# State-space gate: column tiles outside, both halves of y on chip, the y·silu(z) product formed earlier, and two PSUM banks for the attention's filler

## The chip, the cores and the metric

The kernel runs on one core of one Trainium2 chip. Its time is the device time of one execution in microseconds (us), from runs that alternate between the kernels compared; lower is better. TensorE (PE) does the matmuls, VectorE (DVE), ScalarE (ACT) and GpSimd (POOL) the elementwise work, and SyncE (SP) issues the DMAs. "Span" is the time from the first to the last instruction in one profiled execution.

## The reference

One decoder layer on x of 1024 tokens × 2048 channels, all in float32. The part that the change touches is the state-space gate and what reads it.

```python
h = rms_norm(x, ln_gain)
q, k, v, z_att, u, z_ssm, g_att, g_ssm = jnp.split(h @ w_in, splits, axis=-1)
q, k = rms_norm(q, q_norm_gain), rms_norm(k, k_norm_gain)     # per head and map, 64 wide
...
attn = diff_attention(q, k, v, lam)       # 8 heads: softmax(q1 k1) - lam * softmax(q2 k2), causal
y_att = rms_norm(attn, subln_gain) * (1.0 - lam_init) * silu(z_att)
y = gelu(Re(C scan(u)) + d_skip * u)      # 1024 wide
y_ssm = y * sigmoid(y @ w_glu + b_glu)    # the gate, w_glu 1024 x 1024
y_ssm = y_ssm * silu(z_ssm)
merged = sigmoid(g_att) * (y_att @ w_proj_att) + sigmoid(g_ssm) * (y_ssm @ w_proj_ssm)
x = x + merged @ w_out
```

## The kernel before

Every float32 product is made of three matmuls: each operand is split into a high part (ACT, `split`, line 90) and a low part (DVE or POOL, line 91), and high·high, high·low and low·high are summed in PSUM. Tiles have 128 partitions × 512 columns; tokens come in two halves `t` of 512. Intermediate results go through DRAM buffers (`d_yg` holds y, `d_zs` silu(z_ssm), `d_ys` the gate's result in two parts, `d_k` the raw keys, `d_ks` their normalised parts).

In order of time, the program has these stages. Times are from the span's start.

- To 1060 us: half of the input projection (`part`), together with the scan that makes y and stores it to `d_yg`.
- 1060 to 1741.5 us: the other half, 36 column pairs (`whole`, line 492) in the order q, k, v, za (4 pairs each), zs (4), ga (8), gs (8). A pair is 84 matmuls. DVE and POOL recombine sums with terms reloaded from `d_p` (lines 520, 571 to 582) and combine weights (lines 346, 366); each finished tile goes to an evacuation function. For za and zs that is `evac_gate` (lines 1030 to 1039): ACT takes the sigmoid, POOL multiplies (L1035), SP stores. From the first za pair on, `norms_k` (line 1004 onward) takes a step per pair in program order: load a tile of k (`ks`) and its row factors (`rb`), multiply (DVE, L1015), split, store, 16 steps in all. Its tile has the tag "ks" with one buffer.
- 1741.5 to 1859 us: the gate. For each half t: load and split y's half (`ya`, 8 tiles); for each of 8 column tiles ct: load and split two blocks of `w_glu`, load y (`r`, L1127) and silu(z) (`z`, L1129), multiply them on POOL (L1130), 24 matmuls into `pg` (L1135), sigmoid (ACT, L1137), times r (DVE, L1138), split, two stores to `d_ys` (L1142). Between them `first_head` loads the attention's first head.
- 1859 to 2236 us: attention, 8 heads × 8 blocks of 128 query rows. PE's order is written out by hand: scores `s` (L1178, L1181), and later, at set lags, transposes `tp` (L1203), `values` into `op` (L1215) and `sums_of` into `osm` (L1232). DVE (L1185, L1191 to L1194) and ACT (L1187) do the softmax between them. Into the gaps go `FILL` steps of a filler per block: the matmuls of y_ssm @ w_proj_ssm, 24 for a tile (`ps_tile`, L288), each tile into one bank of PSUM, `ac2`; a tile is emptied by one DVE multiply with `z` (L292). `op` and `osm` take turns in another bank, `tps` "op".
- To 2292 us the filler's rest and its last 3 tiles (`TAIL`), then two full-rate matmul stages to the end.

Outside the hand-written stretch a scheduler sets each engine's order from the program's order, its priorities and its buffers. Every engine runs its own list in order and waits on semaphores. DMAs are all issued by SP, in its order.

Of the kernel before, what the change touches and what calls it, by code (L numbers as in the profile page):

```python
# [19 lines left out]
P = 128  # L20
# [47 lines left out]
def hybrid_block(ctx: ExitStack, tc: tile.TileContext, x_t, x_n, w_t, w_v, w_glu, w_pa, w_ps,  # L68
# [205 lines left out]
    def bank(pool, tag="pc"):  # L274
        return lambda: pool.tile([P, 512], F32, name="pc", tag=tag)
# [20 lines left out]
    def branch_weights():  # L296

        def blocks():
            for n in range(2 * KT):
                for b in range(2):  # L300
                    yield load_w(w_ps[n % KT, :, 4 * b:4 * b + 4], 4, Q if n < 2 * KT - TAIL else V)
        it = blocks()
        queue = [next(it)]

        def take():
            queue.append(next(it, None))
            return queue.pop(0)
        return take
# [17 lines left out]
    with ExitStack() as pa_ctx:  # L326
# [170 lines left out]
        def finish():  # L497

            if pending:
                pending.pop()()  # L500
# [526 lines left out]
            split(hi, lo, tp)  # L1027
            store2([d[h, :, t * 512:(t + 1) * 512] for d in d_vs], hi, lo)

        def evac_gate(dst, silu):  # L1030
# [10 lines left out]
        evacs = {"q": evac_q, "k": evac_k, "v": evac_v, "za": evac_gate(d_za, True), "zs": evac_gate(d_zs, True),  # L1041
                 "ga": evac_gate(d_ga, False), "gs": evac_gate(d_gs, False)}
        first = {kind: i for kind, i, _ in KINDS}
        for i, (kind, n) in enumerate(order):
            f, m = evacs[kind], n - first[kind]
            whole(n, a, 0, lambda c, t, st, f=f, m=m: f(2 * m + c, t, st), qp, None, w)
            w = None
            if n == 8:
                steps = qk_norms()
            if n in (8, 10, 12):  # L1050
                next(steps, None)
            if i == 12:
                ks = norms_k()
            if i >= 12:
                next(ks, None)
        finish()
        ev_ctx.close()
        hp_ctx.close()
# [38 lines left out]
        gl = gl_ctx.enter_context(tc.tile_pool(name="gl", bufs=3))  # L1097
        heads = {}

        def first_head():  # L1100
# [1 line left out]
                yield  # L1102
        head0 = first_head()

        def yg_inputs(t):
            def ld(k, hi, lo):
                r = wp.tile([P, 512], F32, name="ya", tag="value", bufs=2)
                D.dma_start(r, d_yg[k, :, t * 512:(t + 1) * 512])
                split(hi, lo, r)
            return ld  # L1110

        for t in range(2):
            tk = slice(t * 512, (t + 1) * 512)
            ya = act_half(act, yg_inputs(t))
            for ct in range(8):
                for _ in range(2 if 8 * t + ct > 2 else 0):
                    next(head0, None)
                ws = []
                for b in range(2):
                    raw = wp.tile([P, 4, P], F32, name="w_raw", tag="w_raw", bufs=5)  # L1120
                    D.dma_start(raw, w_glu[ct, :, 4 * b:4 * b + 4])
                    m = (2 * ct + b) % 7
                    hi, lo = (wp.tile([P, 4, P], F32R, name=n, tag=f"{n}{m}") for n in ("w_hi", "w_lo"))
                    split(hi, lo, raw)
                    ws.append((hi, lo))
                r = gl.tile([P, 512], F32, name="r", tag="r")
                D.dma_start(r, d_yg[ct, :, tk])  # L1127
                z = gl.tile([P, 512], F32, name="z", tag="z")
                D.dma_start(z, d_zs[ct, :, tk])  # L1129
                Q.tensor_tensor(r, r, z, ALU.mult)  # L1130
                ps = acc.tile([P, 512], F32, name="pg", tag="acc")
                for k in range(8):
                    wh, wl = (x[:, k % 4] for x in ws[k // 4])
                    for n, (x, y) in enumerate(((wh, ya[0][k]), (wh, ya[1][k]), (wl, ya[0][k]))):
                        T.matmul(ps, lhsT=x, rhs=y, start=(k == 0 and n == 0), stop=(k == 7 and n == 2))  # L1135
                sg = gl.tile([P, 512], F32, name="sg", tag="sg", bufs=2)
                A.activation(sg, ps, AF.Sigmoid, bias=sm[:, C_BGLU + ct:C_BGLU + ct + 1])  # L1137
                V.tensor_tensor(r, r, sg, ALU.mult)  # L1138
                hi, lo = (gl.tile([P, 512], F32R, name=n, tag=n, bufs=2) for n in ("yh", "yl"))
# [3 lines left out]
                if t == 1 and ct == 5:  # L1143
                    ps_weights = branch_weights()
        run(head0)
        gl_ctx.close()

# [4 lines left out]
    ssq = const.tile([P, H, NT], F32, name="ssq")  # L1152
    with ExitStack() as at:
        at.enter_context(kq_ctx.pop_all())
        pex = at.enter_context(tc.tile_pool(name="pex", bufs=2))
        wtp = at.enter_context(tc.tile_pool(name="wtp", bufs=1))
        osp = at.enter_context(tc.tile_pool(name="osp", bufs=2))
        tiny = at.enter_context(tc.tile_pool(name="tiny", bufs=6))
        ssp = at.enter_context(tc.tile_pool(name="ssp", bufs=2, space=PSUM))
# [77 lines left out]
        def put(i, f):  # L1237
            late.append((i, f))
            late.sort(key=lambda a: a[0])

        def drain(i):
            while late and late[0][0] <= i:
                late.pop(0)[1]()

        def filler():
            psa0 = act_half(act, finished(d_ys, 0))
            for ct in range(KT):
                yield from ps_tile(0, ct, psa0, bank(ac2), ps_weights)
            psa.append(act_half(act, finished(d_ys, 1)))
            for ct in range(KT - TAIL):  # L1250
                yield from ps_tile(1, ct, psa[0], bank(ssp, "s") if ended and ct % 2 else bank(ac2), ps_weights)

        psa, ended = [], []
        fill = filler()
# [3 lines left out]
        def feed(n):  # L1258

            owed[0] += n  # L1260
            while owed[0] > 0:
                owed[0] -= 1
                if next(fill, 0):
                    return
        with tc.manual_schedule(engines={T.engine}):
            for h in range(H):
                ld = heads.get(h) or load_head(h)
                wts = [[wtp.tile([P, 4 * qb + 4, 512], F32R, name=n, tag=f"{n}{qb}") for n in ("wth", "wtl")]
                       for qb in range(2)]
                for n, tt in enumerate(ORDER):  # L1270
                    i = h * NT + n
                    qb = tt // 4
                    w = weights(i, h, tt, ld)
                    q = FILL[n]
                    put(i + LAG_T, lambda a=(tt, w, wts[qb]): transpose_w(*a))
                    if tt % 4 == 3:
                        def vals(i=i, h=h, qb=qb, wt=wts[qb], ld=ld):
                            sq = values(h, qb, wt, ld)
                            put(i + LAG_V + LAG_S, lambda: sums_of(h, qb, sq))
                        put(i + LAG_V, vals)  # L1280
                    drain(i + 0.1)
                    feed(q - q // 2)
                    drain(i + 0.5)
                    feed(q // 2)
                    drain(i + 0.9)
            ended.append(1)
# [153 lines left out]
```

## Time and profile before

| | us |
|---|---|
| median of 3 runs (2804.27 to 2805.68) | 2805.34 |
| the profiled execution | 2804.28 |
| its span | 2802.5 |
| PE busy in the span | 2695.5 (96%) |
| DVE, ACT, POOL busy | 1844.1, 1205.9, 743.7 |
| gate, 1741.5 to 1859: length, PE busy | 117.5, 100.41 |
| from za's first pairs to zs's last, 1250 to 1452: length, PE busy | 202, 180.00 |
| ga and gs, 1452 to 1741.5: length, PE busy | 289.5, 289.50 |

PE's busy time is modelled from pipelined matmuls, so a busy PE may still run at half rate; the granted clock says so. Idle time is told with the instruction that ended it and the one that released it.

### The profile page before, as it was taken

The page shows a single profiled execution, that of the slowest core. Times are in us where ns is not written, and L with a number is a line of the kernel's source. Part 1 is how long each engine was busy: PE and PEld are TensorE (multiplying, and loading weights), DVE is VectorE, ACT ScalarE, POOL GpSimd, SP SyncE. Part 2 cuts the span into 40 slices and gives each one's busy share as a digit, 9 for nine tenths or more (in the row PEclk, how much of TensorE's full clock was granted, in tenths as well). Part 3 has the DMA queues.
Part 4 walks back from the last instruction along what each step waited for, and adds up shares of the span by engine and source line. Part 5 has one row for each costly group of instructions (what it writes and reads, how often), then busy time and mean ns, then how long its engine had stood idle before and what let it go on. Part 6 is the DMA issues. An engine that isn't in the chain of part 4 may idle for free. (4 is left out here: it accounts for less than half of the span.)

```text
span 2802.5 us, 37947 instructions
## 1 busy us (share of the span) xinstructions
PE 2695.5 (96%) x12402; PEld 2205.5 (79%) x12402; DVE 1844.1 (66%) x3512; ACT 1205.9 (43%) x2359; POOL 743.7 (27%) x1101
## 2 busy tenths in 40 slices
PE   9999999999999998998899999789999999999999
PEld 8888788887878876776678888667878778888887
DVE  4998877777787776787676666457666575325432
ACT  6433455545455544433444444345555433223221
POOL 0002866565674011224442222212222200000000
PEclk9999999999999999999999999999999999999999
DMA  9653333333333454457765555976777386455453
GB/s 350 220 180 115 103 113 117 115 116 120 121 101 117 166 181 165 149 174 230 243 214 167 168 162 169 317 234 194 198 238 206 128 296 194 131 155 177 150 158 113
DMA packets 261926, 487.82 MB, mean 174 GB/s; under 512 B 33912, under 2 KB 44480, under 8 KB 261728
## 3 DMA queue, kind: packets, MB, share of 16 engines
q1 hardware_dynamic: 261728, 485.40, 53.7%
q8 instruction: 98, 1.61, 0.2%
q14 instruction: 100, 0.82, 0.1%
HBM read 345.72 MB, written 139.56 MB: 173 GB/s over the span
## 5 line engine op out<-in xcount | busy, mean ns | idle before, releaser
L492 PE MATMUL acc<-ah,w_hi 128*128 128x512 f32 x2128 | 841.6, 396 | 28.1 <-ACT u L523 22.8
L492 PE MATMUL acc<-ah,w_lo 128*128 128x512 f32 x2128 | 841.0, 396 | 0.0
L492 PE MATMUL acc<-al,w_hi 128*128 128x512 f32 x2128 | 840.2, 395 | 0.0
L90 ACT ACTIVATE w_hi<-w_raw 128x512 fp32r<-128x512 f32 x532 | 333.9, 629 | 523.3 <-PE o L1356 219.7
L91 DVE TENSOR_TENSOR w_lo<-w_raw,w_hi 128x512 fp32r<-128x512 f32 x474 | 338.4, 715 | 308.9 <-ACT w_hi L90 296.3
L492 PEld LDWEIGHTS acc<-ah,w_hi 128*128 128x128 f32 x2128 | 402.7, 189 | 120.6 <-ACT u L523 27.6
L492 PEld LDWEIGHTS acc<-ah,w_lo 128*128 128x128 f32 x2128 | 402.5, 189 | 87.7 <-issue 5.4
L492 PEld LDWEIGHTS acc<-al,w_hi 128*128 128x128 f32 x2128 | 402.9, 189 | 83.4 <-issue 2.0
L90 ACT ACTIVATE w_hi<-value 128x512 fp32r<-128x512 f32 x304 | 191.7, 630 | 313.3 <-DVE value L346 161.4
L91 DVE TENSOR_TENSOR w_lo<-value,w_hi 128x512 fp32r<-128x512 f32 x304 | 219.5, 722 | 61.3 <-ACT w_hi L90 53.7
L1356 PE MATMUL o<-w_lo,mh 128*128 128x512 f32 x512 | 199.2, 389 | 0.0
L1356 PE MATMUL o<-w_hi,ml 128*128 128x512 f32 x512 | 199.2, 389 | 0.0
L1356 PE MATMUL o<-w_hi,mh 128*128 128x512 f32 x512 | 195.3, 389 | 0.0
L581 POOL TENSOR_TENSOR u<-u,q 128x512 f32<-128x512 f32 x72 | 99.8, 1387 | 230.2 <-ACT u L514 120.7
L346 DVE TENSOR_TENSOR value<-w_raw 128x512 f32<-128x512 f32 x152 | 150.3, 989 | 2.7
L1185 DVE TENSOR_SCALAR_CACHE_REDUCE pe<-s,nrq 128x128 f32<-128x128 f32 (+7 forms) x128 | 100.1, 813 | 70.9 <-PE s L1181 58.9
L91 POOL TENSOR_TENSOR w_lo<-w_raw,w_hi 128x512 fp32r<-128x512 f32 x58 | 84.0, 1448 | 234.3 <-ACT w_hi L90 204.0
L575 POOL TENSOR_TENSOR p<-p,q 128x512 f32<-128x512 f32 x36 | 60.5, 1680 | 322.5 <-DVE acc L520 210.0
L288 PE MATMUL pc<-ah,w_hi 128*128 128x512 f32 x256 | 107.6, 420 | 25.4 <-DVE z L292 16.8
L1187 ACT ACTIVATE pe<-pe,mx 128x128 f32<-128x128 f32 (+7 forms) x128 | 98.5, 773 | 42.2 <-DVE pe L1185 42.0
L1356 PEld LDWEIGHTS o<-w_lo,mh 128*128 128x128 f32 x512 | 96.1, 188 | 20.0
L1356 PEld LDWEIGHTS o<-w_hi,mh 128*128 128x128 f32 x512 | 96.1, 188 | 19.9
(681 smaller groups left out, 4588.5 us busy)
## 6 DMA issues: line engine op xcount, KB each, us to landing
w_raw<-in_w_t_dram SPq DMA_DIRECT2D x288, 256.0 KB
q<-d_p SPq DMA_DIRECT2D x160, 256.0 KB
w_raw<-in_w_out_dram SPq DMA_DIRECT2D x128, 256.0 KB
d_p<-u SPq DMA_DIRECT2D x72, 256.0 KB
w_raw<-in_w_ps_dram SPq DMA_DIRECT2D x64, 256.0 KB
w_raw<-in_w_pa_dram SPq DMA_DIRECT2D x64, 256.0 KB
d_p<-ps SPq DMA_DIRECT2D x52, 256.0 KB
d_p<-p SPq DMA_DIRECT2D x36, 256.0 KB
```

The costliest lines, as they stand in the source:

```text
L90: A.activation(hi, src, AF.Copy)
L91: (eng or V).tensor_tensor(lo, src, hi.bitcast(F32), ALU.subtract)
L288: T.matmul(ps, lhsT=w[:, k % 4], rhs=b[k], start=(k == 0 and n == 0), stop=(k == 7 and n == 2))
L346: V.tensor_tensor(t, x, y, ALU.add)
L492: T.matmul(ps, lhsT=x[:, c], rhs=y[i][j], start=(start and j == 0 and n == 0), stop=(j == 3 and n == 2), skip_group_check=True)
L575: e.tensor_tensor(u, u, other(1), ALU.add)
L581: e.tensor_tensor(u, u, other(i), ALU.subtract)
L1185: V.tensor_scalar(pc[c][:, 0:w], sc[c][:, 0:w], nrq[:, 2 * h + c, tt:tt + 1], None, ALU.mult, ALU.min, accum_out=mx[:, c:c + 1])
L1187: ins = A.activation(pc[c][:, 0:w], pc[c][:, 0:w], AF.Exp, bias=mx[:, c:c + 1], scale=-1.0, accum_out=su[:, c:c + 1])
L1356: T.matmul(ps[i], lhsT=a[k][:, tt], rhs=w[:, 0], start=(k == 0 and n == 0), stop=(k == KT - 1 and n == 2))
```

## The change

Four things, beside a longer list of names:

1. The evacuation of zs also loads y from `d_yg` (a tile "y" in the one buffer "ks") and multiplies on DVE, so that `d_zs` holds y·silu(z). The gate then loads one tile per step in place of two, and POOL's multiply there goes.
2. In the gate ct is the outer loop and t the inner: each block of `w_glu` is loaded and split once. Both halves of y stay on chip, the second in the attention's q, k and v tiles (`pairs`), split into them before the loop. The first weights and the first half of y are written ahead of the last evacuations (`finish()`).
3. The filler's tiles take turns between `ac2` and the bank "op", the latter only at steps where no `values` or `sums_of` is near; `give_bank` finishes a tile that still holds it. After the last head they alternate between the score banks and `ac2`. `FILL` falls from 76 to 74 per head; the 16 steps left over run after the last head.
4. The pool `wtp` is opened before `pex`, so that the two lie at other addresses.

```diff
-FILL = (10, 9, 10, 9, 10, 9, 10, 9)
+FILL = (10, 9, 9, 9, 10, 9, 9, 9)
...
                     A.activation(sg, st, AF.Sigmoid)
+                    if src is not None:
+                        y = stg.tile([P, 512], F32, name="y", tag="ks", bufs=1)
+                        D.dma_start(y, src[i, :, t * 512:(t + 1) * 512])
+                        V.tensor_tensor(st, st, y, ALU.mult)
                     Q.tensor_tensor(st, st, sg, ALU.mult)
...
+        ahead = gate_weights(0)
+        ya = act_half(act, yg_inputs(0, lambda: wp.tile([P, 512], F32, name="ya", tag="value", bufs=2)))
         finish()
...
-        for t in range(2):
-            tk = slice(t * 512, (t + 1) * 512)
-            ya = act_half(act, yg_inputs(t))
-            for ct in range(8):
-                for _ in range(2 if 8 * t + ct > 2 else 0):
+        pairs = [kq.tile([P, 2, 512], F32R, name="y2", tag=x) for x in
+                 ("qs0", "kh0", "kl0", "qs1", "kh1", "kl1", "vh", "vl")]
+        ya = [ya, ([x[:, 0] for x in pairs], [x[:, 1] for x in pairs])]
+        load = yg_inputs(1, lambda: gl.tile([P, 512], F32, name="ya", tag="ya", bufs=4))
+        for k in range(8):
+            load(k, ya[1][0][k], ya[1][1][k])
+        for ct in range(8):
+            ws, ahead = ahead, gate_weights(ct + 1) if ct < 7 else None
+            for t in range(2):
+                tk = slice(t * 512, (t + 1) * 512)
+                if 2 * ct + t > 1:
                     next(head0, None)
...
-                r = gl.tile([P, 512], F32, name="r", tag="r")
-                D.dma_start(r, d_yg[ct, :, tk])
-                z = gl.tile([P, 512], F32, name="z", tag="z")
-                D.dma_start(z, d_zs[ct, :, tk])
-                Q.tensor_tensor(r, r, z, ALU.mult)
+                r = gl.tile([P, 512], F32, name="r", tag="r", bufs=3)
+                D.dma_start(r, d_zs[ct, :, tk])
...
+        wtp = at.enter_context(tc.tile_pool(name="wtp", bufs=1))
         pex = at.enter_context(tc.tile_pool(name="pex", bufs=2))
-        wtp = at.enter_context(tc.tile_pool(name="wtp", bufs=1))
...
+        def filler_bank():
+            turn[0] ^= 1
+            if ended:
+                return bank(ssp, "s")() if turn[0] else bank(ac2)()
+            own[0] = bool(turn[0]) and (at_step[0] < NT - 2 or not 0.2 < at_step[0] % NT < 4.3)
+            return bank(tps, "op")() if own[0] else bank(ac2)()
...
+        def give_bank():
+
+            while own[0]:
+                owed[0] -= 1
+                step()
...
                         def vals(i=i, h=h, qb=qb, wt=wts[qb], ld=ld):
+                            give_bank()
                             sq = values(h, qb, wt, ld)
-                            put(i + LAG_V + LAG_S, lambda: sums_of(h, qb, sq))
+                            put(i + LAG_V + LAG_S, lambda: (give_bank(), sums_of(h, qb, sq)))
```

Three places show what this does to the engines' lists.

DVE in the zs pairs, before. `value` and `w_lo` prepare weights, `u2`, `u3`, `p1` and `q` are the tiles that an evacuation takes:

```order
L346 TENSOR_TENSOR value_14648<-w_raw_14620,w_raw_14624 128x512
L91 TENSOR_TENSOR w_lo_14651<-value_14648,w_hi_14650 128x512
L1015 TENSOR_TENSOR ks_16167<-ks_16167,rb_16169 128x512
L346 TENSOR_TENSOR value_14812<-w_raw_14800,w_raw_14802 128x512
L582 TENSOR_TENSOR u3_14592<-acc_14566,u3_14592 128x512
L91 TENSOR_TENSOR sl__16334<-ks_16167,sh__16333 128x512
L91 TENSOR_TENSOR w_lo_14809<-w_raw_14802,w_hi_14808 128x512
L576 TENSOR_TENSOR p1_14496<-acc_14498,p1_14496 128x512
```

And after:

```order
L582 TENSOR_TENSOR u3_14427<-acc_14401,u3_14427 128x512
L91 TENSOR_TENSOR w_lo_14659<-w_raw_14652,w_hi_14658 128x512
L1038 TENSOR_TENSOR u3_14427<-u3_14427,y_14433 128x512
L1015 TENSOR_TENSOR ks_14445<-ks_14445,rb_14447 128x512
L576 TENSOR_TENSOR p1_14322<-acc_14324,p1_14322 128x512
L91 TENSOR_TENSOR w_lo_14494<-value_14472,w_hi_14493 128x512
L91 TENSOR_TENSOR sl__14632<-ks_14445,sh__14631 128x512
L346 TENSOR_TENSOR value_14664<-value_14662,w_raw_14654 128x512
L582 TENSOR_TENSOR u2_14337<-acc_14401,u2_14337 128x512
L91 TENSOR_TENSOR w_lo_14498<-w_raw_14462,w_hi_14497 128x512
L91 TENSOR_TENSOR w_lo_14667<-value_14664,w_hi_14666 128x512
L1038 TENSOR_TENSOR p1_14322<-p1_14322,y_14547 128x512
```

Each zs pair has four multiplies by y (L1038) and one step of `norms_k` (L1015, `sl`) in DVE's list, 22 instructions from one `u3` to the next, and these five loads share one buffer. Before, all 16 steps of `norms_k` stood in the za and zs pairs; now 4 stand in za, 4 in zs and 8 in ga.

DVE at the gate's end, with what an instruction waits for, before: the last product with the sigmoid (L1138), its split, and the first softmax (L1185).

```order
L91 TENSOR_TENSOR yl_18391<-r_18357,yh_18390 128x512 [waits DMAHW4_49,Activation_49]
L1138 TENSOR_TENSOR r_18408<-r_18408,sg_18438 128x512 [waits Activation_49,Pool_49]
L91 TENSOR_TENSOR yl_18442<-r_18408,yh_18441 128x512 [waits DMAHW7_49,Activation_49]
L1185 TENSOR_SCALAR pe_18480,mx_18483<-s_18484,nrq_11008 128x640 [waits DMAHW3_49,DMAHW4_49,DMAHW2_49,DMAHW5_49,DMAHW1_49,DMAHW6_49,DMAHW0_49,DMAHW7_49,DVE_49,PE_49]
L1185 TENSOR_SCALAR pe_18481,mx_18483<-s_18485,nrq_11008 128x640 [waits PE_49]
```

And after:

```order
L91 TENSOR_TENSOR yl_18300<-r_18269,yh_18299 128x512 [waits DMAHW4_49,Activation_49]
L1151 TENSOR_TENSOR r_18307<-r_18307,sg_18334 128x512 [waits DMAHW5_49,Activation_49]
L1198 TENSOR_SCALAR pe_18376,mx_18379<-s_18380,nrq_11008 128x640 [waits PE_49]
L91 TENSOR_TENSOR yl_18338<-r_18307,yh_18337 128x512 [waits DMAHW4_49,Activation_49]
L1198 TENSOR_SCALAR pe_18377,mx_18379<-s_18381,nrq_11008 128x640 [waits PE_49]
```

The first softmax tile no longer waits for eight DMA semaphores (they guarded the gate's buffers, at whose address `pe` lay).

SP at the start of the attention's sixth head, before. `qs`, `kh`, `kl` and `vh`, `vl` are that head's tiles, `ah` and `al` the second half of the gate's result for the filler:

```order
L1068 DMA qs_20732<-d_q1_74 64x1024
L293 DMA d_ps_89<-z_20522 128x512
L97 DMA w_raw_20871<-in_w_ps_dram 128x512
L314 DMA al_20793<-d_ys1_88 128x512
L314 DMA ah_20785<-d_ys0_87 128x512
L314 DMA ah_20786<-d_ys0_87 128x512
L314 DMA al_20794<-d_ys1_88 128x512
L314 DMA ah_20787<-d_ys0_87 128x512
L314 DMA al_20795<-d_ys1_88 128x512
L1068 DMA kh_20733<-d_k0_75 64x1024
L1068 DMA kl_20734<-d_k1_76 64x1024
```

And after:

```order
L1092 DMA qs_20612<-d_q1_74 64x1024
L97 DMA w_raw_20749<-in_w_ps_dram 128x512
L293 DMA d_ps_89<-z_20452 128x512
L1092 DMA kh_20613<-d_k0_75 64x1024
L1092 DMA kl_20614<-d_k1_76 64x1024
L314 DMA ah_20714<-d_ys0_87 128x512
L314 DMA al_20722<-d_ys1_88 128x512
```

The head's last `kh` and `kl` are issued ahead of all the 16 loads of the filler's second half instead of behind six of them.

## Rows read from the trace of the kernel before

**Rows 1.** The page, section 1: busy us of each engine (share) xinstructions.

```profile
PE 2695.5 (96%) x12402; PEld 2205.5 (79%) x12402; DVE 1844.1 (66%) x3512; ACT 1205.9 (43%) x2359; POOL 743.7 (27%) x1101
```

**Rows 2.** Busy time by stretch; its second line names the columns.

```profile
core 0: us, PE busy (x) PEld busy (x) DVE busy (x) ACT busy (x) POOL busy (x), PEclk, DMA share, GB/s
1250.00:1370.00 120.00, 105.10 (x446) 82.71 (x445) 88.85 (x126) 45.27 (x81) 46.71 (x30) 0.96 0.72 233
1370.00:1452.00 82.00, 74.90 (x318) 60.02 (x317) 62.32 (x76) 34.38 (x62) 40.09 (x28) 0.98 0.72 235
1452.00:1741.50 289.50, 289.50 (x1279) 239.69 (x1278) 185.93 (x245) 128.73 (x215) 64.01 (x45) 1.00 0.52 166
1741.50:1859.00 117.50, 100.41 (x410) 77.84 (x408) 58.32 (x75) 46.20 (x79) 31.01 (x21) 0.94 0.87 281
1859.00:1880.00 21.00, 11.81 (x46) 8.73 (x47) 7.06 (x17) 4.94 (x11) 1.50 (x1) 0.76 0.70 243
```

**Rows 3.** Waits of PE, 1741.5 to 2300: us in total, times, longest.

```profile
PE pc L288 <- DVE z L292: 16.8, 8, 5.0
PE pg L1135 <- ACT w_hi L90: 11.2, 4, 9.8
PE s L1178 <- DVE pe L1185: 7.8, 1, 7.8
PE pc L288 <- DVE sums L1191: 5.4, 2, 2.7
PE s L1178 <- issue: 5.1, 1, 5.1
PE pg L1135 <- ACT ah L90: 4.7, 3, 3.3
```

**Rows 4.** Groups of PE in the gate: shapes xcount | busy us, mean ns | idle before.

```profile
L1135 PE MATMUL pg<-ah,w_hi 128*128 128x512 f32 x128 | 50.1, 411 | 15.9 <-ACT w_hi L90 11.2 <-ACT ah L90 4.7
L492 PE MATMUL acc<-ah,w_lo 128*128 128x512 f32 x9 | 3.5, 389 | 0.0
```

**Rows 5.** DMA in the gate, in 40 equal slices: busy tenths, GB/s.

```profile
DMA  8658696799999999999999999999992007995996
GB/s 268 185 187 250 245 405 219 215 255 273 344 218 306 282 232 307 267 335 391 391 364 354 382 361 342 402 395 381 313 342 103 0 0 257 323 320 188 349 303 181
```

**Rows 6.** Groups of DVE, 1370 to 1452: shapes xcount | busy us, mean ns | idle.

```profile
L1015 DVE TENSOR_TENSOR ks<-ks,rb 128x512 f32<-128x512 f32 x6 | 5.1, 847 | 13.5 <-DMA ks<-d_k 5.9 <-DMA q<-d_p 5.7 <-DMA d_zs<-q 1.9
...
L91 DVE TENSOR_TENSOR sl__15818<-ks,sh__15817 128x512 fp32r<-128x512 f32 x1 | 1.8, 1751 | 0.0
...
L91 DVE TENSOR_TENSOR sl__15646<-ks,sh__15645 128x512 fp32r<-128x512 f32 x1 | 0.7, 686 | 0.0
```

**Rows 7.** Waits of DVE, 1250 to 1452: us in total, times, longest.

```profile
DVE ks L1015 <- DMA ks<-d_k: 23.0, 10, 6.1
DVE ks L1015 <- DMA rb<-d_rk: 8.3, 3, 4.8
```

**Rows 8.** Timeline, one load of ks and its use: start, us, what [idle before].

```profile
1380.64 0.46 SPq L1004 DMA_DIRECT2D ks<-d_k  x1
...
1386.06 0.69 DVE L1015 TENSOR_TENSOR ks<-ks,rb 128x512 f32<-128x512 f32 x1 [5.69 <-DMA q<-d_p]
```

**Rows 9.** Timeline of DVE at the attention's first softmax.

```profile
1872.42 0.89 DVE L1185 TENSOR_SCALAR_CACHE_REDUCE pe<-s,nrq 128x640 f32<-128x640 f32 x1 [11.33 <-DMA oz<-d_za]
```

**Rows 10.** Timeline of SP and PE at the start of the sixth head.

```profile
2076.02 0.45 SPq L1068 DMA_DIRECT2D kh<-d_k  x1
...
2084.36 0.76 PE L1178 MATMUL s<-kh,qs 128*128 128x512 f32 x1 [5.14 <-issue]
```

**Rows 11.** Timeline of PE and DVE where a filler tile follows another.

```profile
1945.14 0.48 PE L288 MATMUL pc<-ah,w_lo 128*128 128x512 f32 x1
1948.63 0.47 PE L288 MATMUL pc<-ah,w_hi 128*128 128x512 f32 x1 [3.01 <-DVE z L292]
...
1947.80 0.69 DVE L292 TENSOR_TENSOR z<-z,pc 128x512 f32<-128x512 f32 x1
```

More of the change, by code (lines that the diff above doesn't have):

```diff
@@ L1028, in evac_v, with evac_gate @@
             store2([d[h, :, t * 512:(t + 1) * 512] for d in d_vs], hi, lo)
-        def evac_gate(dst, silu):
+        def evac_gate(dst, silu, src=None):
             def f(i, t, st):
@@ L1039, in evac_gate @@
             return f
-        evacs = {"q": evac_q, "k": evac_k, "v": evac_v, "za": evac_gate(d_za, True), "zs": evac_gate(d_zs, True),
+        evacs = {"q": evac_q, "k": evac_k, "v": evac_v, "za": evac_gate(d_za, True), "zs": evac_gate(d_zs, True, d_yg),
                  "ga": evac_gate(d_ga, False), "gs": evac_gate(d_gs, False)}
@@ L1055, in hybrid_block, with yg_inputs, ld, gate_weights @@
                 next(ks, None)
+        def yg_inputs(t, raw):
+            def ld(k, hi, lo):
+                r = raw()
+                D.dma_start(r, d_yg[k, :, t * 512:(t + 1) * 512])
+                split(hi, lo, r)
+            return ld
+        def gate_weights(ct):
+            ws = []
+            for b in range(2):
+                raw = wp.tile([P, 4, P], F32, name="w_raw", tag="w_raw", bufs=5)
+                D.dma_start(raw, w_glu[ct, :, 4 * b:4 * b + 4])
+                m = (2 * ct + b) % 6
+                hi, lo = (wp.tile([P, 4, P], F32R, name=n, tag=f"{n}{m}") for n in ("w_hi", "w_lo"))
+                split(hi, lo, raw)
+                ws.append((hi, lo))
+            return ws
+        ahead = gate_weights(0)
+        ya = act_half(act, yg_inputs(0, lambda: wp.tile([P, 512], F32, name="ya", tag="value", bufs=2)))
         finish()
@@ L1096, in hybrid_block @@
         gl_ctx = ExitStack()
-        gl = gl_ctx.enter_context(tc.tile_pool(name="gl", bufs=3))
+        gl = gl_ctx.enter_context(tc.tile_pool(name="gl", bufs=2))
         heads = {}
@@ L1133, in hybrid_block @@
                     wh, wl = (x[:, k % 4] for x in ws[k // 4])
-                    for n, (x, y) in enumerate(((wh, ya[0][k]), (wh, ya[1][k]), (wl, ya[0][k]))):
+                    for n, (x, y) in enumerate(((wh, ya[t][0][k]), (wh, ya[t][1][k]), (wl, ya[t][0][k]))):
                         T.matmul(ps, lhsT=x, rhs=y, start=(k == 0 and n == 0), stop=(k == 7 and n == 2))
-                sg = gl.tile([P, 512], F32, name="sg", tag="sg", bufs=2)
+                sg = gl.tile([P, 512], F32, name="sg", tag="sg")
                 A.activation(sg, ps, AF.Sigmoid, bias=sm[:, C_BGLU + ct:C_BGLU + ct + 1])
                 V.tensor_tensor(r, r, sg, ALU.mult)
-                hi, lo = (gl.tile([P, 512], F32R, name=n, tag=n, bufs=2) for n in ("yh", "yl"))
+                hi, lo = (gl.tile([P, 512], F32R, name=n, tag=n) for n in ("yh", "yl"))
                 split(hi, lo, r)
@@ L1142, in hybrid_block @@
                     D.dma_start(d_[ct, :, tk], s_.bitcast(F32))
-                if t == 1 and ct == 5:
-                    ps_weights = branch_weights()
+            if ct == 6:
+                ps_weights = branch_weights()
         run(head0)
@@ L1243, in drain @@
                 late.pop(0)[1]()
+        at_step, turn, own = [0.0], [0], [False]
+        def filler_bank():
[4 more added lines that the diff above has]
+            return bank(tps, "op")() if own[0] else bank(ac2)()
         def filler():
@@ L1247, in filler @@
             for ct in range(KT):
-                yield from ps_tile(0, ct, psa0, bank(ac2), ps_weights)
+                yield from ps_tile(0, ct, psa0, filler_bank, ps_weights)
             psa.append(act_half(act, finished(d_ys, 1)))
             for ct in range(KT - TAIL):
-                yield from ps_tile(1, ct, psa[0], bank(ssp, "s") if ended and ct % 2 else bank(ac2), ps_weights)
+                yield from ps_tile(1, ct, psa[0], filler_bank, ps_weights)
         psa, ended = [], []
@@ L1262, in feed, with step @@
                 owed[0] -= 1
-                if next(fill, 0):
+                if step():
                     return
+        def step():
+            done = next(fill, 0)
+            if done:
+                own[0] = False
+            return done
+        def give_bank():
+            while own[0]:
+                owed[0] -= 1
+                step()
         with tc.manual_schedule(engines={T.engine}):
@@ L1285, in hybrid_block @@
                     drain(i + 0.9)
+            give_bank()
             ended.append(1)
```

16 lines of the change are left out of this document (2 added, 14 removed).

## The prediction

> **What bounds the kernel now.** I read the page's busy times first: PE is busy for 2695.5 of the 2802.5 us of the span [rows 1], so only the 107 us in which it idles, and the stretches in which it runs at half rate, can be won. The table by stretches shows where they are. From 1452 to 1741.5, PE is busy throughout at the full granted clock, and 1279 matmuls take 289.5 us: 0.2264 us each [rows 2]. That is my price for PE's work. By it the gate's 410 matmuls, 128 of each of three kinds and the last of the projection [rows 4], are worth 92.8 us, and it takes 117.5: 24.7 us are lost there, 17.1 of them idle and the rest at a granted clock of 0.94 [rows 2]. The za and zs pairs from 1250 to 1452 idle 14.9 and 7.1 us, and the attention's first 21 us idle 9.2 [rows 2]. Next, the waits of PE name the releasers in the gate and the attention [rows 3]: DVE's emptying of the filler's bank (the rows for z and for sums: 16.8 and 5.4 us), the gate's weights and inputs (11.2 and 4.7), one wait for the first softmax (7.8) and one of 5.1 us put down to "issue". In the gate the reader should see that the transfers, not an engine, are late: ACT's splits wait, and DMA is 0.9 busy or more from the 9th slice to the 30th, at 350 to 400 GB/s where it is fullest [rows 5].
>
> **The gate: 24.7 us lost become 3.** A step of 24 matmuls is 5.43 us of PE. Before, it moves two blocks of weights, r, z and two stores of 256 KB each, 1.57 MB, which is 290 GB/s; in the steps that also carry two loads of the first head it is about 390, all that the fullest slices show [rows 5]. After, a column tile with both halves (10.9 us) moves two blocks, two loads and four stores, 2.10 MB or 193 GB/s, and some 240 with the head's loads. So PE sets the pace once the stage runs. Its start costs something: the second half of y is eight loads and eight splits (0.69 to 1.75 us each on DVE, [rows 6]), and SP and DVE do them while PE has the first half's first two column tiles, 10.9 us, as cover. Should the cover fail, one wait like the 4.7 us for inputs [rows 3] returns. I take 3 us: minus 22, between minus 24 and minus 12. POOL's multiply goes too, but nobody on the path waited for POOL, so I count nothing for it.
>
> **The zs pairs and the steps of norms_k: plus 7.** Here the change adds work: 16 loads and 16 DVE multiplies. The DMA side has room (0.72 busy, [rows 2]); DVE has not. It is busy 62.32 us in 76 instructions, 0.82 us each, in a stretch of 82 us [rows 2]. The new list has 22 instructions per zs pair: 18.0 us. A step of norms_k makes DVE wait as well, 23.0 and 8.3 us over 16 steps, 2.0 each [rows 7]. Each y goes into the one buffer that the previous y or ks has just left, so its load can start only behind that multiply; three or four DVE instructions (2.5 to 3.3 us) stand between two multiplies. A load of this size, issued inside a burst, was usable 5.4 us later [rows 8]. The new ones are issued one by one, so I take 4 us, which leaves a wait of 0.9 us each. Queued behind a waiting multiply are DVE's weight parts and the additions that empty PSUM, so PE waits for both. Together 18.0 + 2.0 + 3.6 = 23.6 us per pair against 84 × 0.2264 = 19.0 for PE: 4.6 lost, 18 in four pairs. Now the 16 steps stand in za and zs, where PE idles 14.9 + 7.1 = 22.0 us, 1.4 per step [rows 2]. Four stay in za: 5.5. Eight move to ga, where PE never waits and DVE is 64% busy [rows 2]: between nothing and 11, I take 5.5. Sum 29 against 22: plus 7. If the y waits vanish it is 4 + 5.5 + 0 − 22 = minus 12; if each load takes the 5.4 us of [rows 8], the waits are 2.5 each and the sum is plus 38.
>
> On the price of one multiply there is a row and a rule. DVE's instructions with two tiles in SBUF as inputs take 0.69 us or up to 1.75, and 0.85 on average for ks [rows 6]; POOL is 49% busy beside them [rows 2]. The Trainium skill (SBUF — State Buffer, "Who interferes with whom") says that such a DVE instruction and a GpSimd instruction that reads SBUF exclude each other for their whole length. The trace agrees in that both values occur. Taken at its worst it is the fourth rival.
>
> **The attention's start: minus 8.** The first softmax on DVE began at 1872.42 after 11.3 us of idling put down to a DMA [rows 9]; the listing of what it waits for shows eight DMA semaphores, and PE's next scores waited 7.8 us for it [rows 3]. The listing of the changed kernel has PE alone there. The stretch idles 9.2 us and its clock falls to 0.76 [rows 2]; I expect about 10 us back, less up to 2 because the last piece of the gate's first half is now stored at the very end, just ahead of the filler's need for it. Between minus 10 and minus 4.
>
> **The sixth head: minus 6.** A `kh` was issued at 2076.02, and the scores that need it started at 2084.36 after 5.14 us of idling; that first matmul took 0.76 us [rows 10] against 0.47 for one at the full clock [rows 11]. It stood behind six loads of the filler's second half. Those now come behind it, so the wait goes, with about 1 us of half rate. Nothing else was late there. Bounds 0 and minus 8.
>
> **The filler's bank: minus 10.** A tile that starts right behind another one needs the bank that DVE has not emptied. At 1945.14 a tile's last matmul starts, DVE reaches the multiply at 1947.80, behind two softmax instructions, and the next tile starts at 1948.63, 3.01 us of idling [rows 11]. Waits of this kind are nine of the ten in the rows for z and sums; 22.2 us in all, less 5.0 for the one at the end, 17.2 [rows 3]. With two banks in turn a tile finds the other one empty. But the second is barred around `values` and `sums_of`, and by the order of PE's list about half of the direct starts still fall on the bank just used. Half of 17.2 is 8.6, and with the half-rate matmuls behind the long ones 10. Bounds 0 and minus 17. FILL's 16 matmuls move behind the last head, where they cost PE the same: nothing, covered by nothing.
>
> **The end of the filler: minus 3.** The one wait of 5.0 us for z [rows 3] has ten more matmuls ahead of it, 2.3 us, and the two banks. Bounds 0 and minus 5.
>
> **Sum.** 7 − 22 − 8 − 6 − 10 − 3 = −42. The profiled execution took 2804.28 us, 1.1 below the median of 2805.34, so 2762.3 and, at the median, **2763 us**.
>
> **The rivals.** *First, the other side: the one buffer sets zs's pace.* Twenty uses (16 y, 4 ks) go through it in turn. If a use costs 5.4 us of load [rows 8], a multiply at 1.75 [rows 6] and 0.9 for SP's turn behind a store that waits for POOL, it is 8 us, 160 for the stage. Four pairs now take 82 × 336 / 318 = 86.6 us. So zs gains 73, za loses 8 and ga gains 5: plus 70 in place of plus 7, and 2826 us. It decides against the change from 6.9 us per use on. For it: the loads are strictly serial, and DVE already waits for ks in 10 of 16 steps. Against it: those loads sat in bursts, and DMA is not full there.
> *Second: the gate stays starved.* If its waits come from SP's order rather than the volume (a store that waits for DVE holds the loads behind it), half the loss stays, 12 us in place of 3: 2772. For it, slices with 185 to 250 GB/s early in the stage [rows 5]; against it, the 22 full slices.
> *Third: the softmax takes over.* PE's waits for the filler's bank give DVE time; without them the scores may wait for DVE instead, and the 10 us come back: 2773. For it, the multiply stood behind softmax work in [rows 11].
> *Fourth: DVE and POOL exclude each other in zs.* Sixteen multiplies at 1.75 in place of 0.69 are 17 us more on DVE: 2780.
>
> **How the numbers follow.** Forecast 0.45, first rival 0.08, second 0.15, third 0.14, fourth 0.13, and 0.05 that zs hides its new work entirely (2744). Below, the range takes in that case with the filler's other bound: 2737. Above, it takes in the second to fourth rivals and most of the plus 38 bound: 2795. The first rival is left out. 0.2% (5.6 us) is about what a measurement of this kernel can tell from no change. Near 6.9 us per use the first rival passes through "same". Faster 0.90, same 0.03, slower 0.07.
>
> **What would show it right or wrong.** A gate of about 95 us with DMA under 0.8 and a few us of waits for weights and inputs; the 7.8 us for the softmax and the 5.1 at the sixth head gone; z and sums near 10 us in place of 22; the zs pairs near 95 us with DVE waiting for y about 1 us each time, and a few us of idling in ga. I am wrong if zs takes over 120 us, or if PE's waits in the attention only change their names.

## The result and the profile after

The changed kernel takes 2775.09 us (median of 4 runs, 2772.23 to 2779.85) beside 2804.81 for the kernel before (4 runs, 2803.65 to 2805.68). The ratio is 0.9896, with a 95% interval of 0.9879 to 0.9913: by the ratio 29 us faster where 42 were forecast, inside the range. The profiled execution has a span of 2773.9 us against 2802.5.

The table by stretches, for the kernel after. Its columns are those of [rows 2]. The first three stretches are za, zs and the half of ga with the last eight steps of `norms_k`, cut near the ends of their evacuations; then come the gate and the attention's first 21 us.

```profile
core 0: us, PE busy (x) PEld busy (x) DVE busy (x) ACT busy (x) POOL busy (x), PEclk, DMA share, GB/s
1290.00:1368.00 78.00, 73.02 (x313) 59.01 (x312) 61.05 (x71) 31.11 (x56) 38.74 (x27) 0.98 0.64 210
1368.00:1457.00 89.00, 76.58 (x314) 60.14 (x312) 66.08 (x81) 30.49 (x54) 34.84 (x24) 0.96 0.66 209
1457.00:1545.00 88.00, 78.49 (x312) 62.80 (x313) 57.94 (x81) 36.25 (x64) 17.64 (x12) 0.92 0.72 235
1754.50:1854.00 99.50, 95.62 (x410) 77.10 (x408) 39.42 (x59) 37.45 (x63) 6.24 (x5) 0.98 0.87 265
1854.00:1875.00 21.00, 19.29 (x105) 16.45 (x106) 15.23 (x38) 12.33 (x27) 4.16 (x3) 1.00 0.93 268
```

One row of the kernel before that was not shown ahead of the prediction, the za pairs:

```profile
1290.00:1370.00 80.00, 66.41 (x265) 51.66 (x264) 54.73 (x71) 30.21 (x54) 30.82 (x22) 0.94 0.72 228
```

A stretch's length less 0.2264 us per matmul, the prediction's price, is what it loses. Before, 1290 to 1452 loses 80 − 265 × 0.2264 = 20.0 and 10.0 us [rows 2], 30 in all. After, za loses 7.1, zs 17.9 and ga, which lost nothing, 17.4: 42.4. The gate has 410 matmuls in both and loses 6.7 in place of 24.7. The attention's first 21 us idle 1.7 in place of 9.2, and the clock there is 1.00 instead of 0.76. What that is worth can be read directly: from the first scores to those of the third block of queries PE has the same list in both kernels, and takes 19.2 us before and 6.7 after.

```profile
1858.95:1878.14 19.19, 9.99 (x35) 7.14 (x36) 5.23 (x15) 4.94 (x11) 0.62 (x1) 0.73 0.73 255
1853.91:1860.64 6.73, 6.73 (x35) 5.76 (x36) 4.91 (x14) 5.06 (x11) 0.89 (x1) 1.00 0.97 348
```

What PE waited for after that, 1741.5 to 2300 (us in total, times, longest), to be read beside [rows 3]:

```profile
PE pc L288 <- ACT w_hi L90: 6.4, 1, 6.4
PE pc L288 <- DVE z L292: 5.2, 3, 3.0
PE s L1191 <- DMA kl<-d_k: 3.4, 6, 0.7
PE pg L1148 <- ACT y L90: 2.7, 1, 2.7
PE tp L1216 <- DVE wtl L91: 2.5, 2, 2.0
...
PE s L1191 <- DVE pe L1207: 1.5, 1, 1.5
PE s L1191 <- DMA kh<-d_k: 1.3, 2, 0.8
PE op L1228 <- DVE z L292: 1.2, 1, 1.2
```

The weights of the gate (11.2), the first softmax (7.8) and the "issue" at the sixth head (5.1) are gone, and z and sums fell from 22.2 to 5.2. New are one long wait for w_hi and a few on the softmax side (wtl, pe, op); short waits for kl and kh are eight, where there were three for kl.

What DVE waited for from 1250 to 1545, beside [rows 7]:

```profile
DVE ks L1015 <- DMA ks<-d_k: 31.3, 11, 5.6
DVE ks L1015 <- DMA rb<-d_rk: 13.0, 4, 5.0
DVE p L1038 <- DMA y<-d_yg: 6.5, 4, 1.7
DVE ks L1015 <- DMA d_ga<-p: 5.5, 1, 5.5
...
DVE u L1038 <- DMA y<-d_yg: 1.8, 4, 0.7
```

PE does not wait for that multiply itself. In the half of ga (1457 to 1545) all that it waits for is ACT's copy of a PSUM bank (L523, the tile `u3`):

```profile
PE acc L492 <- ACT u L523: 11.1, 4, 4.1
```

One of the four shows the chain. DVE's multiply waits for ks; ACT's split of its result waits for DVE; the copy stands behind that split in ACT's list; and PE starts when the copy ends:

```profile
1503.97 0.69 DVE L1015 TENSOR_TENSOR ks<-ks,rb 128x512 f32<-128x512 f32 x1 [2.90 <-DMA ks<-d_k]
1504.75 0.63 ACT L90 ACTIVATE sh__16037<-ks 128x512 fp32r<-128x512 f32 x1 [4.40 <-issue]
1505.90 0.58 ACT L523 ACTIVATE u<-acc 128x512 f32<-128x512 f32 x1
1506.53 0.79 PE L492 MATMUL acc<-ah,w_hi 128*128 128x512 f32 x1 [4.11 <-ACT u L523]
```

### The profile page after: what moved, and what is told of

Same layout as the page of the kernel before. It is cut to its first block, busy times and chain, and to the rows that moved or that the text cites. A ratio compares the mean times of both kernels' runs of the same rounds, so it can differ in the third digit from the quotient of the medians.

```text
span 2773.9 us, 37831 instructions
## 1 busy us (share of the span) xinstructions
PE 2688.6 (97%) x12402; PEld 2203.8 (79%) x12402; DVE 1837.8 (66%) x3512; ACT 1195.8 (43%) x2343; POOL 714.7 (26%) x1085
## 4 chain that ended last, share of the span: by engine, by line
PE 77%; DMA 9%; DVE 7%; ACT 2%; issue 2%; POOL 2%; SPq 1%; DVEq 0%; ACTq 0%; POOLq 0%
PE acc L492 40%; PE o L1395 12%; PE pc L271 6%; PE pc L288 4%; PE acc L476 3%; PE pg L1148 2%; PE op L1228 2%; PE s L1191 1%; DVE w_lo L91 1%; DMA ks<-d_k 1%; DMA kl<-d_k 1%; DMA w_raw<-in_w_ps_dram 1%; DMA ya<-d_yg 1%; DMA y<-d_yg 1%; PE tp L1216 1%
## 5 line engine op out<-in xcount | busy, mean ns | idle before, releaser
L90 ACT ACTIVATE w_hi<-w_raw 128x512 fp32r<-128x512 f32 x516 | 323.8, 629 | 520.0 <-PE o L1395 234.1
L91 DVE TENSOR_TENSOR w_lo<-w_raw,w_hi 128x512 fp32r<-128x512 f32 x458 | 327.2, 715 | 297.6 <-ACT w_hi L90 289.3
L91 DVE TENSOR_TENSOR w_lo<-value,w_hi 128x512 fp32r<-128x512 f32 x304 | 226.0, 744 | 58.5 <-ACT w_hi L90 50.7
L1395 PEld LDWEIGHTS o<-w_hi,ml 128*128 128x128 f32 x512 | 96.2, 188 | 19.8
```

What stands on the lines that cost most here:

```text
L1395: T.matmul(ps[i], lhsT=a[k][:, tt], rhs=w[:, 0], start=(k == 0 and n == 0), stop=(k == KT - 1 and n == 2))
```

## The experiments

All times are medians; the kernel before, run beside them on the same chip, is given with each.

### The four parts, each alone on the kernel before (before: 2803.54)

The first part, zs's product without the new loop of the gate:

```diff
-"zs": evac_gate(d_zs, True),
+"zs": evac_gate(d_zs, True, d_yg),
...
-                D.dma_start(r, d_yg[ct, :, tk])
-                z = gl.tile([P, 512], F32, name="z", tag="z")
-                D.dma_start(z, d_zs[ct, :, tk])
-                Q.tensor_tensor(r, r, z, ALU.mult)
+                D.dma_start(r, d_zs[ct, :, tk])
```

> The kernel before with the first part alone: y is loaded and multiplied in zs's evacuation through the shared buffer, and the gate, still with t outside, loads one tile per step and has no POOL multiply. If the added work in zs and the norms_k steps pushed into ga cost what the trace of the changed kernel shows (46.8 us lost between 1250 and 1545 against 34.5 before), that stretch gives +12; if the gate was bound by the volume of its transfers (1.57 to 1.31 MB per step), the gate's 25 us of loss shrink to about 15: -10. Sum +2, between -3 and +7. Rival: the gate was starved by the order of SP's list, not by volume; then the gate stays and the sum is +12.

2804.57 us, ratio 1.0004 (0.9991 to 1.0017). The gate's first matmul came 7.6 us later than before (1749.1 against 1741.5) and the first scores 1.9 us earlier (1857.1 against 1859.0), so the gate gave back what zs had cost. The theory's sum came out, with a smaller cost ahead of the gate than the 12 expected: the gate moved 29.2 MB in place of 33.0 and lost 15.2 us in place of 24.7. POOL's multiply left the gate in the same edit, so the volume alone is not shown to be the cause. PE's long wait for the gate's weights stayed:

```profile
PE pg L1136 <- ACT w_hi L90: 8.6, 1, 8.6
```

The second, the gate's new loop with the old two loads and POOL's multiply in it (the lines as they differ from the changed kernel):

```diff
                 D.dma_start(r, d_yg[ct, :, tk])
+                z = gl.tile([P, 512], F32, name="z", tag="z")
+                D.dma_start(z, d_zs[ct, :, tk])
+                Q.tensor_tensor(r, r, z, ALU.mult)
```

> The kernel before with the second part alone: ct outside, both halves of y on chip, weights split once, the first weights and half written early; r and z are still loaded and multiplied on POOL in the gate. Theory: the volume falls from 1.57 to 1.31 MB per 5.4 us, and PE has two steps per pair of weight blocks: the gate loses about 7 to 10 us instead of 25, -15 to -18, and nothing else changes. Rival: without the fewer r loads the gate stays starved: -8 or less.

2789.61 us, ratio 0.9948 (0.9931 to 0.9966), 14 us. The gate moved 28.0 MB, nearly as much as with the first part alone, at a DMA share of 0.93, and lost 7.2 us; the waits for its weights are gone. So some 8 us of the gate's gain come with the order of the loop and of its loads, and not with the volume. "Nothing else changes" was wrong, though: behind the shorter gate PE waited longer for the first softmax than the 7.8 us of [rows 3]. PE's waits from 1835 to 1865:

```profile
PE s L1194 <- DVE pe L1201: 10.4, 1, 10.4
PE s L1194 <- ACT sg L1153: 3.5, 1, 3.5
```

The third, the banks:

```diff
-                yield from ps_tile(0, ct, psa0, bank(ac2), ps_weights)
+                yield from ps_tile(0, ct, psa0, filler_bank, ps_weights)
```

> The kernel before with the third part alone: two banks in turn for the filler, FILL 74. Theory: the waits for the bank fall from about 22 to 10 us, -10 to -13 with the half-rate matmuls behind them. Rival: the softmax takes over, the scores wait for DVE instead: -4 or less.

2792.64 us, ratio 0.9963 (0.9951 to 0.9974), 10 us: the theory's lower end.

The fourth, the order of the two pools:

```diff
+        wtp = at.enter_context(tc.tile_pool(name="wtp", bufs=1))
         pex = at.enter_context(tc.tile_pool(name="pex", bufs=2))
-        wtp = at.enter_context(tc.tile_pool(name="wtp", bufs=1))
```

> The kernel before with the fourth part alone: wtp is opened before pex, so the first softmax no longer waits for the gate's stores. Theory: the 7.8 us wait of the scores goes, with about 1.5 us of half rate: -8 to -10. Rival: the waits go to the first transposed weights instead and PE loses the same time some 10 us later: -3 or less.

2799.76 us, ratio 0.9989 (0.9976 to 1.0001): 3 us, not clear of no change, near the rival's size but not by its mechanism. The wait for the softmax is gone from PE's waits (1855 to 1885), and nothing waits for the transposed weights; the filler's inputs, which come through DMA behind the gate's last stores, are late instead:

```profile
PE pc L288 <- DMA al<-d_ys: 2.2, 3, 1.2
PE pc L288 <- DMA ah<-d_ys: 1.3, 3, 0.5
```

In the whole change the stretch won 7.5 us of idling. That the gate has less to transfer at its end there is a likely reason; no run shows it apart.

The four ratios add up to −0.96%, and the whole is −1.04%. That does not make the parts independent. These are us against the kernel before, from one profiled execution each: how much later the gate's first matmul starts, then the change in the time from it to the first scores, from the first to the last scores, and from there to the end.

| | to the gate | gate | first to last scores | rest |
|---|---|---|---|---|
| first part | +7.6 | −9.5 | −1.8 | −0.2 |
| second | −1.0 | −17.5 | +6.4 | −2.7 |
| third | +3.3 | +0.4 | −12.6 | +0.7 |
| fourth | +0.2 | −1.6 | −0.4 | −0.4 |
| their sum | +10.1 | −28.2 | −8.4 | −2.6 |
| the whole | +13.0 | −18.1 | −23.7 | +0.1 |

The third part and the whole put some 15 of the filler's matmuls, 3.4 us, off into the last stretch. Kernels that are alike up to the gate differ there by up to 3.4 us. In the gate the first and second parts do not add up: the four together win 10 us less than one by one. In the attention they win 15 us more. The two about cancel. With the second part in place, the first buys the gate next to nothing (99.4 us against 100.0), and the gate starts 14 us later with it (1754.5 against 1740.5). A kernel with the other three alone was not run, so what the first part does for the attention's start is open.

### What the zs pairs and norms_k cost

The first three are made on the changed kernel; beside the first two the kernel before took 2803.77 us, beside the others 2802.80. The changed kernel's own ratio is 0.9896. A buffer of its own for y:

```diff
-                        y = stg.tile([P, 512], F32, name="y", tag="ks", bufs=1)
+                        y = stg.tile([P, 512], F32, name="y", tag="y", bufs=1)
```

> The changed kernel with a buffer of its own for y, so that y and ks no longer share one; norms_k's steps then stand where they stood before the change, in za and zs. Theory: sharing costs DVE its 8.3 us of waits for y and lengthens the waits for ks (49.8 us of DVE after, 38.9 before): the stretch from 1250 to the last projection matmul loses about 40 us in place of 47.6, -5 to -9. Rival: the 11 us of new DVE work is what costs; the sharing is not, and the time stays within 2 us.

2770.95 us, ratio 0.9884 (0.9863 to 0.9905): 3 us less than the changed kernel, not clear of noise. The profiled span is 6 us shorter, and the gate's first matmul starts at 1745.9 in place of 1754.5, so sharing cost about 8 us up to there, as the theory had it, and the attention gave some back (330.8 us from the first to the last scores against 327.7). All 16 steps of norms_k stand in za and zs again, so the 8 us are for the wait at the shared buffer and for the move into ga together.

Two buffers for ks and y, and two for rb:

```diff
-                st = stg.tile([P, 512], F32, name="ks", tag="ks", bufs=1)
+                st = stg.tile([P, 512], F32, name="ks", tag="ks", bufs=2)
...
-                rb = stg.tile([P, 512], F32, name="rb", tag="rb", bufs=1)
+                rb = stg.tile([P, 512], F32, name="rb", tag="rb", bufs=2)
...
-                        y = stg.tile([P, 512], F32, name="y", tag="ks", bufs=1)
+                        y = stg.tile([P, 512], F32, name="y", tag="ks", bufs=2)
```

> The changed kernel with two buffers for ks (and y, which shares them) and two for the row factors rb, so that a load can be issued while the one before it is in use. Theory: DVE's waits for ks, rb and y (58 us together) are single loads in series behind one buffer; with two they mostly go, and the stretch from 1250 loses 20 to 27 us in place of 47.6: -20 to -27. Rival: DVE's work (busy 0.74 of the zs stretch) and the DMA queue set the pace anyway: -8 or less.

2745.14 us, ratio 0.9791 (0.9772 to 0.9810): 29 us less, a little past the theory. The gate's first matmul starts at 1722.1, 32 us earlier. DVE's waits at ks, 58 us in the changed kernel with those for y, are 11 here, and there are none for y (1250 to 1545):

```profile
DVE ks L1015 <- DMA rb<-d_rk: 4.0, 4, 1.3
DVE ks L1015 <- DMA ks<-d_k: 3.9, 5, 1.0
...
DVE ks L1015 <- issue: 3.0, 1, 3.0
```

ks and y alone, rb with one buffer as before:

> The changed kernel with two buffers for ks (and y), rb left with one. rb can be loaded only behind the multiply that used the one before it, so if loads in series are the cause, half of the serial loads stay: the stretch loses about 30 us in place of 47.6 (16.9 with both doubled), -13 to -20. Rival: only the loads of ks and y count, rb comes early enough: -27 to -30, as with both.

2752.36 us, ratio 0.9825 (0.9804 to 0.9845): 20 us less, the theory's upper end. DVE still waits for rb, 12.3 us in 8 times.

The same two doublings, of ks and rb, on the kernel before:

> The kernel before, none of the change in it, with two buffers for ks and two for rb. If the 35 us that it loses from 1250 to the last projection matmul are norms_k's loads in series behind one buffer, most of it goes: the stretch loses 8 to 15, -20 to -27, about 2779 us. Its difference from the changed kernel with two buffers (16.9 us lost there) is then the price of the 16 loads and multiplies by y alone. Rival: the doubled buffers help only where y shares them: -8 or less.

2790.37 us, ratio 0.9954 (0.9938 to 0.9971): 12 us where 20 to 27 were expected, a miss. DVE's waits for ks and rb went there too:

```profile
DVE ks L1015 <- DMA rb<-d_rk: 3.7, 3, 2.0
DVE ks L1015 <- DMA ks<-d_k: 1.9, 2, 1.0
```

but all 16 steps of norms_k now stand in the za pairs and the start of zs, three to a pair, and the gate starts at 1727.9, 5.8 us later than in the changed kernel with the same buffers. So the extra loads and multiplies by y cost nothing that can be seen once no load waits behind one buffer. What the steps cost in the kernel before was only in part their loads; the rest is not explained.

### The attention's new waits, and a faster kernel

The loads of each head, tied to marks one block earlier:

```diff
-                    after(ins, marks[(h - 1) * NT + 1 + i // 2])
+                    after(ins, marks[(h - 1) * NT + i // 2])
```

> The changed kernel with each head's loads tied to marks one block earlier in the head before. Theory: PE's short waits for kl and kh at the start of seven heads (4.7 us, 1.6 before the change) come from loads that arrive late now that PE is faster; one block (some 5 us) earlier they are there: -3 to -5 with the half-rate matmuls behind them. Rival: the earlier loads push the filler's weights and inputs back in the same queue: within 1 us of no change.

2767.07 us (before 2803.77), ratio 0.9868 (0.9845 to 0.9891): 8 us less than the changed kernel, more than expected. The two intervals just overlap, but from the first to the last scores it takes 318.5 us in place of 327.7. From 1870 to 2180 PE waits for kl once, and no longer for kh, pe or sums:

```profile
PE pc L288 <- DVE z L292: 3.5, 3, 1.4
PE s L1191 <- DMA kl<-d_k: 1.7, 1, 1.7
PE op L1228 <- DVE z L292: 1.2, 1, 1.2
PE pc L288 <- ACT wth L90: 1.1, 1, 1.1
PE tp L1216 <- DVE wtl L91: 0.5, 1, 0.5
```

The filler's last weights at high priority:

```diff
+                        if n >= 2 * KT - TAIL - 1:
+                            hp.enter_context(tc.high_priority())
```

> The changed kernel with the filler's last weight loads at high priority, which puts one of them ahead of two loads of pf (SP is held at the first pf until d_f has landed). Theory: the wait of 6.4 us for w_hi near the filler's end is the weights standing behind pf in SP's list: they land some 2 to 3 us earlier, -2 to -3. Rival: pf itself is what the next stage needs, and comes later by as much: no change.

2777.99 us (before 2803.77), ratio 0.9908 (0.9888 to 0.9927): no gain, as the rival had it. The trace of the changed kernel shows why:

```profile
2228.11 0.69 DVE L1361 TENSOR_TENSOR pr<-pr,pf 128x512 f32<-128x512 f32 x1 [5.28 <-DMA pf<-d_f]
...
2231.86 0.68 DVE L292 TENSOR_TENSOR z<-z,pc 128x512 f32<-128x512 f32 x1
...
2232.03 0.63 ACT L90 ACTIVATE w_hi<-w_raw 128x512 fp32r<-128x512 f32 x1 [0.57 <-DMA w_raw<-in_w_ps_dram]
...
2232.69 0.77 PE L288 MATMUL pc<-ah,w_hi 128*128 128x512 f32 x1 [6.39 <-ACT w_hi L90]
```

Two things come ready together: w_hi is split until 2232.66, and the bank is emptied (z, L292) until 2232.54. In the new kernel w_hi ends at 2232.41, and PE still starts only behind z:

```profile
2232.97 0.68 DVE L292 TENSOR_TENSOR z<-z,pc 128x512 f32<-128x512 f32 x1
...
2233.80 0.77 PE L288 MATMUL pc<-ah,w_hi 128*128 128x512 f32 x1 [6.04 <-ACT ah L90]
```

The step held up is z: PE starts 0.15 us after it in both kernels, and 0.14 after it in [rows 11]. The `ah` to which the profile puts the second wait down is split from `pr`, for the next stage, and this matmul does not read it. z stands in DVE's list behind multiplies of pr by pf, the first of which waits 5.28 us for its transfer.

The two gains together, doubled buffers and earlier heads:

> The changed kernel with two buffers for ks, y and rb and with each head's loads one block earlier. Theory: the two causes lie in different stages, so their gains add (-30 and -8 against the changed kernel's 2775): about 2737 us. Rival: the heads' loads, now in a faster stream, collide with the filler's, and half of the second gain goes: 2741 or more.

2736.34 us (before 2802.80), ratio 0.9760 (0.9745 to 0.9775): 38 us less than the changed kernel, so they add. From the first to the last scores it takes 317.9 us, against 330.0 with the doubled buffers alone.

That with the multiply by pf moved to POOL for the first half:

```diff
-            V.tensor_tensor(r, r, f, ALU.mult)
+            (V if t else Q).tensor_tensor(r, r, f, ALU.mult)
```

> The kernel with doubled ks, y, rb and earlier heads, and the multiply pr times pf for the first half moved from DVE to POOL, which is idle there. Theory: the 6.9 us wait for z at the filler's end is DVE held, in its order, by a multiply that waits for pf, with z behind it; on POOL the wait holds neither, only al<-pr still stands ahead of z on DVE, and the wait shrinks by 2 to 4 us: -2 to -4 against 2736. Rival: what is late is pf, whoever multiplies by it; POOL takes 1.4 us where DVE takes 0.7, and the time stays or grows.

2732.52 us (before 2803.48), ratio 0.9741 (0.9727 to 0.9754). The median is 4 lower, but the intervals overlap, and the wait at which it was aimed, z from 2150 to 2240, went only from 6.9

```profile
PE pc L288 <- DVE z L292: 6.9, 1, 6.9
```

to 6.3:

```profile
PE pc L288 <- DVE z L292: 6.3, 1, 6.3
```

On DVE the split of pr (al) still stands ahead of z and waits for the same transfer, so the rival is right about that wait. Whether the 4 us are real, and from where, stays open.

## Why the prediction was right, and where it was off

The direction and the places were right; 42 us were forecast and 29 came, and the sizes of the steps were off both ways. By its own steps:

- **The gate**: −22 forecast, −18 measured (24.7 lost, now 6.7), inside its bounds. The cover of the start fell short: PE waited 2.7 us for the split of a tile of the second half, and from 1778.2 to 1787.6 the granted clock was 0.82. One step was wrong without harm: the transfers did not become light, as the sign "DMA under 0.8" had it. They move 26.4 MB in place of 33, in a shorter stage, at 265 GB/s and 0.87 busy:

```profile
DMA  8888979999999999999999999999818072638699
GB/s 294 252 254 287 323 241 344 186 243 278 359 250 222 194 214 212 242 355 385 331 365 336 395 355 278 302 288 349 274 69 268 16 236 81 231 117 187 228 399 373
DMA packets 13396, 26.40 MB, mean 265 GB/s; under 512 B 1567, under 2 KB 1567, under 8 KB 13389
```

  I had counted the loop's loads and stores and the head's loads, and forgotten that y's second half (10 loads of y fall in the stage) and the filler's first inputs (14) share it. So light transfers are not what lets PE set the pace. The second rival had named part of the cause, the order: the first and second parts alone move 29.2 and 28.0 MB, and only with the second, which asks for the next weights a column tile ahead, are the waits for them gone.
- **zs and norms_k**: +7 forecast, +12 measured. The zs pairs themselves came out as worked: 89 us for 314 matmuls are 23.8 us per pair against 23.6. That is partly luck: the y waits were smaller (8.3 us in 8 of 16 uses, not 14), the ks waits longer (13.6 us for four steps, not 8). The term that was mis-sized is ga's: the eight steps of norms_k that moved there cost 17.4 us where I took 5.5 and thought 11 the most. 9.5 of them are idle, the rest is a clock of 0.92. DVE had room on average, at 64% busy, but it works in order: it waits for ks 23.6 us in eight times, and not the additions alone stand behind that wait, as I had it, but ACT's splits and, behind them, the copies that free PSUM for PE (11.1 us of PE's waits). My price of 1.4 us per step counted idle time only, and 30 us were lost there before, not 22; that error ran the other way and hid more than half of the first. (The bound of plus 38 holds with ga at its 11 us; with 5.5 it is 33.)
- **The attention's start**: −8 forecast, −12 measured (19.2 us, now 6.7, for the same work), past the bound of −10: with the idling gone, the half rate behind it went too. The cause is not the fourth part by itself, as I had it: alone it removed the wait and left the time from the first to the last scores as it was (351.0 us against 351.4).
- **The sixth head**: its 5.1 us are gone, as forecast.
- **The filler's bank**: the waits for z and sums were 17.2 us without the last [rows 3], and are 6.4 (z 5.2, op on z 1.2): minus 11, against 8.6 forecast. But the third rival took part of it back, with the heads' loads beside the softmax: waits for kl and kh went from 1.6 to 4.7, and short ones for pe, sums and wtl appeared. From the first to the last scores the attention won 23.7 us: 12.4 at its start, 3.4 by the 15 filler matmuls put off, and 8 where I had put 16 for this step and the sixth head. Tying the loads earlier won 9 more.
- **The end of the filler**: −3 forecast. The wait itself grew: 5.0 for z became 6.4 put down to w_hi. I followed PE's list and the banks, and not what stands ahead of z in DVE's. Yet from the last scores to the end the two kernels take the same time (592.3 and 592.2 us) with 15 matmuls more, 3.4 us, in the new one: two waits for the bank behind the last scores, 3.0 and 1.0 us before, are gone. So the size came about, but not at the wait that I named: that is luck.

Of the rivals, the first did not come about: 23.8 us per pair are five uses of the buffer, 4.8 us each at most, under the 6.9 from which it decides. The second did not come about in size (6.7 us lost, not 12), though part of its cause did, as said above. The third was right in part. The fourth fell: all 16 multiplies by y took 0.68 to 0.70 us, though POOL was busy for 34.84 of zs's 89 us. That does not settle whether the two hold each other up: for 13 of the 16, POOL stood idle and waited for that very result. These are minimum, median and maximum of each group, in ns:

```profile
L1038 DVE TENSOR_TENSOR u<-u,y x8: 693/693/695, 1363.0 to 1452.7; 128x512 f32<-128x512 f32 x8
L1038 DVE TENSOR_TENSOR q<-q,y x4: 676/679/691, 1354.2 to 1432.6; 128x512 f32<-128x512 f32 x4
L1038 DVE TENSOR_TENSOR p<-p,y x4: 691/692/694, 1374.0 to 1449.4; 128x512 f32<-128x512 f32 x4
```

## What to carry to other kernels

Work that is moved to an engine with idle time can cost that engine's waits and not only its busy time: count the loads that wait one behind the other at a single buffer, what stands behind them in the engine's list, and what the next engine's list then holds back. Here a second buffer was worth as much as the whole change. A removed stall shows the next one in the same stage, so ask of each what is late next: in the attention it was the heads' loads, and tying them one block earlier won 8 us more. And parts whose times add up need not be independent: compare them stage by stage.

## What the runs showed of the hardware

The DMA queues were 0.87 busy in the gate before and after, with slices at 330 to 399 GB/s in the changed kernel; PE lost 24.7 us before and 6.7 after, and 7.2 in the second part alone at 0.93. So a full queue alone does not say that a stage is bound by it. DVE's two-input multiplies ran at their short duration all 16 times in a stage in which POOL was 39% busy, but in 13 of them POOL was waiting for the result, while a split nearby in the kernel before took 1.75 us [rows 6]; which pairs of instructions slow each other was not tried.
